# Operand scales from a ones matmul on TensorE in place of GpSimd's maximum over partitions

## The chip, the cores and the metric

The kernel runs on one core of a Trainium2 chip. The metric is the device time of one execution, in microseconds. Five engines work from instruction rows of their own: TensorE (PE, with its weight loads shown apart as PEld), VectorE (DVE), ScalarE (ACT), GpSimd (POOL) and SyncE (SP), which here issues most of the transfers.

## What is computed

One layer of a hybrid backbone over 2048 latent tokens of width 1024, with 256 context tokens, all float32:

```python
mod = silu(c) @ w_ada + b_ada                    # six shifts, scales and gates
h = rms_norm(x, norm1_g) * (1 + scale) + shift   # same for the context tokens
u, g, p, gt = split(h @ w_in)                    # LRU, GeLU gate, pool branch, branch gates
uc = depthwise_conv(u)
r, i = sigmoid(uc @ w_r + b_r), sigmoid(uc @ w_i + b_i)   # both directions, per head
out = scan(a(r), b(r, i, uc))                    # forward and backward, context state first
m = sigmoid(gt1) * ((out * gelu(g)) @ w_lru_out) + sigmoid(gt2) * (pool_mixer(p) @ w_pool_out)
x = x + gate * (m @ w_o)
h2 = rms_norm(x, norm2_g) * (1 + scale2) + shift2
x = x + gate2 * (square(relu(h2 @ w1)) @ w2)
y = rms_norm(x, final_g)
```

## The kernel before

Channels lie on the 128 partitions, tokens on the free dimension, in blocks of 512 tokens (b = 0 to 3). A float32 product is made of three float16 passes (`mm3`, L67 to L72, its matmuls are `mm` at L72): each operand is multiplied by a power of two, `s`, and split into a high and a low half (`split`, L93 to L95: the high half by ACT at L94, the low half by DVE at L95). The inverse scale goes into the evacuation.

The power of two comes from the operand's magnitude. DVE reduces each partition (`absmax`, L91, into `wm` for a weight chunk, `um` for an activation; two chunks that share a scale are joined into `wmj` at L114). `scale_of_` (L79 to L88) then makes one number of the 128: L81 is the maximum over partitions on POOL, into `sc_g`, L83 takes the exponent on DVE, L85 and L87 make the inverse `sc_inv` and the scale `sc_s`. There are 122 such calls: 69 for `wm`, 32 for `wmj`, 18 for `um` and 3 for `bd`, the bound of a modulated norm (`affine`, L340). The hidden activations of the MLP have a maximum over partitions of their own (`m1_split`, L837, `hm` at L841, 64 times), which the change leaves alone.

The other work of POOL is elementwise: the sums of squares of the first norms (L257), every second multiply of `modulate` (L237, tile `t` or `slot`), the products of input gates (L498), one step of the scans (L513), the sum of both directions (L535), and in the norms of the second half L217, L220 and L882.

The program runs in stages. The start (0 to 218 us) makes the adaLN vectors, the first norm and the first products. Eight LRU tiles of 128 channels follow (to about 916 us): the convolution (L471), `um` and its split, gate products, the scans (L521, L522), the GeLU gate, and between them, as `between`, the u products of the next tile, whose evacuation is L422, and part of the adaLN sums. Then come the pool branch (to 950), the branch products and the merge (to 1310; it reloads z and y from memory, into `B` and `yw`), the products with w_o and the second norm (`make_h2`, b = 3 last, at 1531 to 1602), and the MLP (16 groups of 256 hidden channels by 4 blocks, to the end), with the weights of the next group prepared meanwhile.

The order on SP is that of the code. On PE, DVE, ACT and POOL a scheduler sets it when the kernel is built, from its own time model; the blocks under `tc.high_priority` (`scale_of`, L76, among them) go first where they can. The order is fixed from then on, and each engine works its row in that order. TensorE's results of small sums, 512 columns at most, go to the PSUM pool `psm` (L60, tile `sm`), which has one buffer: the sum over partitions of squares by a ones matmul (`rstd`, L205), the adaLN sums (L401) and the last norm use it. `ones` (L133) is a 128x128 float32 tile of ones; L321 is a further ones matmul, of adaLN sums, into the pool of products.

Of the kernel before, what the change touches and what calls it, by code (L numbers as in the profile page):

```python
# [7 lines left out]
F32 = mybir.dt.float32  # L8
# [6 lines left out]
DRAM = bass.MemoryType.DRAM  # L15
ABSMAX = bass.bass_isa.ReduceOp.absmax

P = 128
# [3 lines left out]
BW = 512  # L22
# [19 lines left out]
def block_kernel(ctx: ExitStack, tc: tile.TileContext, a):  # L42
    """Activations keep channels on partitions and tokens on the free dimension.

    Matrix products run as three float16 passes (hi*hi + hi*lo + lo*hi) over operands that are
    scaled by powers of two taken from their measured magnitude and split into two halves.
    """
    nc = tc.nc
# [16 lines left out]

    # ---------------------------------------------------------------- helpers
    def mm3(ps, ws, xs):  # L67
# [11 lines left out]
    def scale_of_(m, k):  # L79
        g = sm.tile([P, k], F32, name=f"sc_g{k}")  # L80
        G.partition_all_reduce(g, m, P, ABSMAX)  # L81
        e = sm.tile([P, k], I32, name=f"sc_e{k}")
        V.tensor_scalar(e, g.bitcast(I32), 0x7F800000, None, op0=OP.bitwise_and)  # L83
        inv = sm.tile([P, k], F32, name=f"sc_inv{k}", bufs=8 if k == 1 else 4)
        V.tensor_scalar(inv.bitcast(I32), e, 14 << 23, 20 << 23, op0=OP.subtract, op1=OP.max)  # L85
        s = sm.tile([P, k], F32, name=f"sc_s{k}")
        V.tensor_scalar(s.bitcast(I32), inv.bitcast(I32), -1, 254 << 23, op0=OP.mult, op1=OP.add)  # L87
        return s, inv  # L88
# [13 lines left out]
    def prep(srcs, joint=False, w16=None):  # L102
        """Load chunks [128, n <= 1024]; each gets its own scale, or all of them one."""
        k = len(srcs)
        raws, m = [], sm.tile([P, k], F32, name=f"wm{k}")
        for i, src in enumerate(srcs):
            n = src.shape[-1]
            raw = ring.tile([P, 1024], F32, name="raw")
            nc.sync.dma_start(raw[:, :n], src)
            absmax(m[:, i:i + 1], raw[:, :n])  # L110
            raws.append(raw[:, :n])
        if joint:
            mj = sm.tile([P, 1], F32, name="wmj")
            V.tensor_reduce(mj, m, axis=AX.X, op=OP.max)  # L114
            m = mj
        s, inv = scale_of(m, 1 if joint else k)
        out = []
        for i, raw in enumerate(raws):
            n = raw.shape[-1]
            t = ring.tile([P, 2, 1024], F16, name="w16") if w16 is None else w16[i]  # L120
            split(t[:, 0, :n], t[:, 1, :n], raw, s[:, 0:1] if joint else s[:, i:i + 1])
            out.append(t)
        return out, inv
# [3 lines left out]

    # ---------------------------------------------------------------- constants and vectors
    vec = cp.tile([P, NV], F32, name="vec")
# [21 lines left out]

    # 8*softplus(-lam): max(-lam, 0) + log1p(exp(-|lam|)), log1p(e) = 2 atanh(e / (2 + e))
    nlam = cp.tile([P, 16], F32, name="nlam")
# [22 lines left out]

    # ---------------------------------------------------------------- scratch in DRAM
    z_d = [dram.tile([P, T], F32, name=f"z{j}") for j in range(KT)]
# [6 lines left out]

    # ================================================================ stages 0-3
    st = ExitStack()
# [14 lines left out]
    def rstd(total, w, rs):  # L202
        """1 / sqrt(mean + eps) on every partition of sums of squares [128, w] per partition."""
        ps = psm.tile([P, BW], F32, name="sm")
        TE.matmul(ps[:, :w], ones, total, start=True, stop=True)  # L205
        S.activation(rs, ps[:, :w], AF.Sqrt, bias=eps, scale=1.0 / D)
        V.reciprocal(rs, rs)
        return rs

    def rstd_of(x, w, t_tile):  # L210
        """The same of x [128, 8, w]."""
        acc = None
        for q in range(4):
            sq = ring.tile([P, 2, BW], F32, name="raw")[:, :, :w]
            S.activation(sq, x[:, 2 * q:2 * q + 2, :], AF.Square)
            if q:
                G.tensor_tensor(acc, acc, sq, op=OP.add)  # L217
            else:
                acc = sq
        G.tensor_tensor(acc[:, 0, :], acc[:, 0, :], acc[:, 1, :], op=OP.add)  # L220
        return rstd(acc[:, 0, :], w, t_tile()[:, :w])

    def pair(t, w=BW):
        """[128, k, w] float32 seen as [128, k, 2, w] float16: high and low halves in its place."""
        return t.bitcast(F16).rearrange("p k (h w) -> p k h w", h=2)

    def modulate(x, w, rs, gs, ss, dst, tmp):
        """x [128, 8, w] -> dst [128, 8, 2, w] (may be the same bytes)."""
        for k in range(KT):
            t = tmp()[:, :w]  # L230
            if k % 2 == 0:
                V.scalar_tensor_tensor(t, x[:, k, :], gs[:, k:k + 1], rs, op0=OP.mult, op1=OP.mult)
                S.activation(dst[:, k, 0, :], t, AF.Identity, bias=ss[:, k:k + 1])  # L233
                V.scalar_tensor_tensor(dst[:, k, 1, :], t, ss[:, k:k + 1], dst[:, k, 0, :],
                                       op0=OP.add, op1=OP.subtract)
            else:
                G.tensor_tensor(t, x[:, k, :], rs, op=OP.mult)  # L237
                S.activation(t, t, AF.Identity, bias=ss[:, k:k + 1], scale=gs[:, k:k + 1])
                S.activation(dst[:, k, 0, :], t, AF.Copy)
                V.tensor_tensor(dst[:, k, 1, :], t, dst[:, k, 0, :], op=OP.subtract)  # L240
# [8 lines left out]
    def norm_x(x, w, eng):  # L249
        """Its inverse root mean square and a supply of pieces, both in one slot."""  # L250
        t = slot([P, 4, BW])[:, :, :w]
# [24 lines left out]

    # shift1 and scale1 for the latent and the context stream
    w_ada = a["w_ada"].rearrange("(k p) n -> p k n", p=P)
# [16 lines left out]
    def ada1_pe(wt, cc):  # L295
        """As rows on two partitions, then turned into columns."""
        ps = ptile()
# [10 lines left out]
    def ada1_dve(wt, c):  # L308
        """Products summed over k on VectorE, then over partitions."""
        acc = slot([P, 512])  # L310
        for k in range(KT):
            if k == 0:
                V.tensor_scalar(acc, wt[k], sil[:, k, c:c + 1], None, op0=OP.mult)
            else:
                V.scalar_tensor_tensor(acc, wt[k], sil[:, k, c:c + 1], acc, op0=OP.mult, op1=OP.add)
        return acc
# [23 lines left out]
    def affine(scale, shift, g, m):  # L340
        """Scaled per-channel factor and term of a modulated norm, and the inverse scale."""
        gm = cp.tile([P, KT], F32, name=f"gm{m}")
# [41 lines left out]
    def ada_piece(q):  # L384
        """gate1, shift2, scale2, gate2 (q = 0..3) of the latent stream."""
        acc = slot([P, D])
# [20 lines left out]
    class Fill:  # L407
        """Sigmoid of one tile of branch-gate channels, kept in DRAM for the merge."""

# [23 lines left out]
    class Lru:  # L433
        """One tile of 128 recurrent channels: conv, gates, both scans, gelu gate."""

# [43 lines left out]
        def gates(self, between=()):  # L479
            """Recurrence and input gates; the products of other tiles go in between."""  # L480
            j, uc, u16, g16 = self.j, self.uc, self.u16, self.g16
# [57 lines left out]

    # first tiles, token block by token block as the normed input becomes ready  # L540
    def together(tiles, b):
# [77 lines left out]

    # ---------------------------------------------------------------- pool branch  # L620
    def rows(t, o=8, w=64):
# [73 lines left out]

    # ================================================================ branch outputs and merge
    st = ExitStack()
# [63 lines left out]

    # ================================================================ w_o, residual, second norm
    aff2 = affine(mod2[:, 2, :], mod2[:, 1, :], vc("g2"), 2)
# [47 lines left out]

    # ================================================================ squared-relu mlp
    st2.close()
# [73 lines left out]
    class FinishLast:  # L887
        """The same with the shortest way from the last product to the output."""

# [51 lines left out]

# [1 line left out]
def _tiles(w, cols):  # L943
    """[K, N] -> [128, K/128 * width] for a column range, k-tile major."""
    k, n = w.shape[0] // P, cols[1] - cols[0]
    return w[:, cols[0]:cols[1]].reshape(k, P, n).transpose(1, 0, 2).reshape(P, k * n)
# [54 lines left out]
```

## Time and profile before

| what | us |
|---|---|
| median of three runs | 2885.27 |
| lowest, highest | 2882.92, 2886.13 |
| the profiled execution: span | 2885.5 |
| TensorE busy in it | 2721.1 (94%) |
| DVE busy | 1904.9 (66%) |
| ACT busy | 812.7 (28%) |
| POOL busy | 459.1 (16%) |

The profile is of one execution, and its span lies within the runs. Busy time is summed over the whole span, though the stages differ: TensorE is full from the merge on, but for a few places, and has idle time ahead of it. A row of an instruction gives its start, its length and, in brackets, how long its engine idled before it and what ended that; "issue" is time in which the engine waited for nothing that the profile shows.

### The profile page before, as it was taken

How to read it: one execution, taken by the hardware profiler on the slowest of the kernel's cores; microseconds unless marked ns; L12 is line 12 of the kernel's file. 1: busy time of each engine (PE TensorE's matmuls, PEld its weight loads, DVE VectorE, ACT ScalarE, POOL GpSimd, SP SyncE). 2: the span in 40 equal slices, each digit the busy share in tenths (PEclk: the TensorE clock that was granted, in tenths of full speed). 3: DMA queues.
4: the chain of work that ended last, by engine and by line, in shares of the span. 5: the costliest groups of instructions: out<-in, count | busy, mean ns of one | idle time of the engine just before them, and what ended most of it. 6: DMA issues, size and time to landing. Idle time of an engine off the chain costs nothing.

```text
span 2885.5 us, 30620 instructions
## 1 busy us (share of the span) xinstructions
PE 2721.1 (94%) x12496; PEld 1241.8 (43%) x12496; DVE 1904.9 (66%) x2883; ACT 812.7 (28%) x917; POOL 459.1 (16%) x371
## 2 busy tenths in 40 slices
PE   5798988898889999999997999999999999999998
PEld 1344444444334444444443444444444444444444
DVE  4867778875576745676466666666666665656567
ACT  2655564446545232113231111011011110110112
POOL 2713332332322000000331000000000000000022
PEclk7899999999999999999999999999999999999999
DMA  7021123211111136433001000000000000000002
GB/s 304 9 77 59 70 99 113 88 51 55 55 41 40 55 121 222 154 105 132 30 18 56 30 30 29 16 30 25 20 30 30 30 16 29 30 22 23 0 30 88
DMA packets 49165, 177.60 MB, mean 62 GB/s; under 512 B 4736, under 2 KB 7040, under 8 KB 43520
## 3 DMA queue, kind: packets, MB, share of 16 engines
q1 hardware_dynamic: 44992, 146.29, 14.9%
q10 hardware_dynamic: 4032, 29.36, 2.5%
q8 instruction: 97, 1.59, 0.2%
q14 instruction: 44, 0.36, 0.0%
HBM read 137.88 MB, written 37.75 MB: 61 GB/s over the span
## 4 chain that ended last, share of the span: by engine, by line
PE 66%; DVE 13%; issue 7%; ACT 6%; POOL 5%; DMA 3%; SPq 0%; ACTq 0%; DVEq 0%; POOLq 0%
PE mm L72 65%; DVE slot L515 2%; POOL slot L513 2%; POOL sc_g L81 1%; DMA raw<-z 1%; DVE slot L518 1%; DVE slot L512 1%; DVE slot L395 1%; DVE wm L91 1%; POOL slot L535 1%; ACT slot L493 1%; DVE A L868 1%; DVE slot L471 1%; ACT slot L94 1%; POOL slot L257 1%
## 5 line engine op out<-in xcount | busy, mean ns | idle before, releaser
L72 PEld LDWEIGHTS <-w 128*128 128x128 f16 x10944 | 1078.1, 99 | 1387.2 <-issue 136.9
L72 PE MATMUL mm<-B,w 128*128 128x512 f16 x3840 | 845.6, 381 | 15.1 <-ACT B L233 5.3
L72 PE MATMUL mm<-A,w 128*128 128x512 f16 x3408 | 774.3, 388 | 72.2 <-ACT slot L422 56.8
L72 PE MATMUL mm<-h,w 128*128 128x512 f16 (+1 forms) x3120 | 676.4, 376 | 9.7 <-DVE h L858 9.5
L868 DVE SCALAR_TENSOR_TENSOR A<-mm,cs,A 128x512 f32<-128x512 f32 (+1 forms) x520 | 373.6, 738 | 44.2 <-PE mm L72 42.5
L833 DVE TENSOR_SCALAR_CACHE_REDUCE r<-mm 128x512 f32<-128x512 f32 x128 | 88.2, 689 | 309.8 <-PE mm L72 309.7
L855 ACT ACTIVATE h<-r 128x1024 f16<-128x1024 f32 x64 | 67.6, 1056 | 791.4 <-DVE ivs L850 766.0
L94 ACT ACTIVATE w<-raw,sc_s 128x1024 f16<-128x1024 f32 (+1 forms) x116 | 127.1, 1116 | 458.9 <-PE mm L72 260.2
L91 DVE TENSOR_REDUCE wm<-raw 128x1 f32<-128x1024 f32 (+1 forms) x124 | 146.2, 1181 | 123.9 <-DMA raw<-in_w_dram 78.5
L72 PE MATMUL mm<-B,yw 128*128 128x512 f16 x768 | 166.4, 379 | 0.0
L841 POOL PARTITION_ALL_REDUCE hm<-um x64 | 23.1, 361 | 865.9 <-DVE um L839 841.9
L95 DVE SCALAR_TENSOR_TENSOR w<-raw,sc_s,w 128x1024 f16<-128x1024 f32 (+1 forms) x116 | 143.1, 1253 | 26.7 <-ACT w L94 26.2
L72 PE MATMUL mm<-slot,g 128*128 128x512 f16 (+1 forms) x528 | 118.6, 373 | 4.9 <-ACT slot L493 4.9
L81 POOL PARTITION_ALL_REDUCE sc_g<-wm x69 | 65.6, 973 | 308.6 <-DVE wm L91 249.8
L72 PEld LDWEIGHTS <-yw 128*128 128x128 f16 x768 | 75.1, 98 | 91.6 <-issue 1.7
L493 ACT ACTIVATE slot<-mm,vec,ivg 128x512 f32<-128x512 f32 (+1 forms) x160 | 105.0, 743 | 10.9 <-PE mm L72 9.8
L498 POOL TENSOR_TENSOR slot<-slot 128x2312 f32<-128x2312 f32 x16 | 83.6, 5223 | 117.5 <-ACT slot L493 115.3
L94 ACT ACTIVATE slot<-slot,sc_s 128x2312 f16<-128x2312 f32 (+1 forms) x12 | 25.8, 2148 | 258.9 <-DVE sc_s L87 240.2
L512 DVE SCALAR_TENSOR_TENSOR slot<-slot 128x2312 f32<-128x2312 f32 x16 | 41.0, 2562 | 82.7 <-ACT slot L511 82.7
L72 PE MATMUL mm<-yw,w 128*128 128x512 f16 x384 | 83.4, 379 | 0.3 <-DVE w L95 0.2
L72 PEld LDWEIGHTS <-g 128*128 128x128 f16 x528 | 53.9, 102 | 65.5 <-issue 13.1
L858 DVE TENSOR_TENSOR h<-sq,h 128x1024 f16<-128x1024 f32 x64 | 77.9, 1217 | 0.0
(182 smaller groups left out, 2108.1 us busy)
## 6 DMA issues: line engine op xcount, KB each, us to landing
raw<-in_w_dram SPq DMA_DIRECT2D x64, 512.0 KB, 3.2
slot<-in_w_ada_dram SPq DMA_DIRECT2D x22, 1024.0 KB, 5.5
A<-in_xT_dram SPq DMA_DIRECT2D x8, 2048.0 KB, 8.7
t<-s SPq DMA_DIRECT2D x64, 256.0 KB, 3.5
s<-slot ACTq DMA_DIRECT2D x11, 1024.0 KB, 4.0
raw<-in_w_gt_dram SPq DMA_DIRECT2D x16, 512.0 KB, 7.2
z<-slot ACTq DMA_DIRECT2D x8, 1024.0 KB, 5.4
raw<-z SPq DMA_DIRECT2D x16, 512.0 KB, 5.8
```

The costliest lines, as they stand in the source:

```text
L72: TE.matmul(ps, l, r, start=(c == 0), stop=(c == n - 1))
L81: G.partition_all_reduce(g, m, P, ABSMAX)
L91: V.tensor_reduce(out, x, axis=AX.X, op=OP.max, apply_absolute_value=True)
L94: S.activation(hi, x, AF.Copy, scale=s)
L95: V.scalar_tensor_tensor(lo, x, s, hi, op0=OP.mult, op1=OP.subtract)
L493: S.activation(dst[:, o:o + w], ps[:, :w], AF.Sigmoid, bias=vcol("br" if i == 0 else "bi", 8 * d + j), scale=self.ivg)
L498: G.tensor_tensor(I, I, uc, op=OP.mult)
L512: V.scalar_tensor_tensor(Tt, A, 1.0, Tt, op0=OP.add, op1=OP.mult)
L833: V.tensor_scalar(r[:, i, :], ps, 0.0, None, op0=OP.max, op1=OP.max, accum_out=pm[:, i:i + 1])
L855: S.activation(h16[:, 0], r, AF.Square)
L858: V.tensor_tensor(h16[:, 1], sq, h16[:, 0], op=OP.subtract)
L868: V.scalar_tensor_tensor(x1[b][:, n, c], ps, cs[:, n:n + 1], x1[b][:, n, c], op0=OP.mult, op1=OP.add)
```

## The change

The maximum over partitions in `scale_of_` becomes a matmul of the 128x128 ones with the column of 128 partition maxima. TensorE adds up the maxima, and every partition of the PSUM tile holds the sum. So the scale comes from a sum of 128 magnitudes, which is at least their maximum and at most 128 times it; the rest of the scale's arithmetic is as before and reads PSUM. The tile comes from `psm`, whose one buffer it now shares with the norms' sums, the adaLN sums and the last norm. Comments are dropped elsewhere in the file; nothing else changes.

```diff
@@ scale_of_ (lines 79 to 88)
     def scale_of_(m, k):
-        g = sm.tile([P, k], F32, name=f"sc_g{k}")
-        G.partition_all_reduce(g, m, P, ABSMAX)
+        g = psm.tile([P, BW], F32, name="sm")[:, :k]
+        TE.matmul(g, ones, m, start=True, stop=True)
         e = sm.tile([P, k], I32, name=f"sc_e{k}")
         V.tensor_scalar(e, g.bitcast(I32), 0x7F800000, None, op0=OP.bitwise_and)
```

The change leaves SP's order alone. POOL's row goes from 365 entries to 164 and TensorE's from 24614 to 24736. Three places show the order.

POOL at the second norm of the last block, `make_h2(3)`, before. An ISA row with `sc_g` or `hm` is a maximum over partitions; one that names no tile stands wherever POOL goes over from elementwise work to maxima or back:

```order
L237 ISA
L237 TENSOR_TENSOR t_10237<-A_9481,t_10227 128x512
L81 ISA
L81 ISA sc_g_10948<-wmj 128x1
L237 ISA
L237 TENSOR_TENSOR t_10246<-A_9481,t_10227 128x512
L81 ISA
L81 ISA sc_g_10975<-wmj 128x1
L237 ISA
L237 TENSOR_TENSOR t_10255<-A_9481,t_10227 128x512
L841 ISA
L841 ISA hm<-um 128x1
```

The same place after:

```order
L841 ISA
L841 ISA hm<-um 128x1 x2
L237 ISA
L237 TENSOR_TENSOR t_10237<-A_9481,t_10227 128x512
L237 TENSOR_TENSOR t_10246<-A_9481,t_10227 128x512
L237 TENSOR_TENSOR t_10255<-A_9481,t_10227 128x512
L237 TENSOR_TENSOR t_10264<-A_9481,t_10227 128x512
L841 ISA
L841 ISA hm<-um 128x1 x57
```

The four multiplies of L237 stand together now, and the maxima of weights between them are gone.

TensorE at the first LRU tile, before: `w_1088` is the weight of fill products, `g_1108` that of the first gate products, which need the split of `um`'s operand:

```order
L72 MATMUL mm<-A_358,w_1088 128x512
L72 LDWEIGHTS g_1108
L72 MATMUL mm<-slot,g_1108 128x512
L72 LDWEIGHTS g_1108
L72 MATMUL mm<-slot,g_1108 128x512
L72 LDWEIGHTS g_1108
L72 MATMUL mm<-slot,g_1108 128x512
```

The same place after, where `um` and four `wm` are columns of partition maxima:

```order
L72 LDWEIGHTS w_1088
L72 MATMUL mm<-A_358,w_1088 128x512
L81 MATMUL sm<-um,ones 128x1
L81 MATMUL sm<-wm_1249,ones 128x1
L81 MATMUL sm<-wm_1529,ones 128x1
L81 MATMUL sm<-wm_1544,ones 128x1
L81 MATMUL sm<-wm_1562,ones 128x1
L72 LDWEIGHTS g_1108
L72 MATMUL mm<-slot,g_1108 128x512
L72 LDWEIGHTS g_1108
```

Five ones matmuls, `um` and four of weights, now stand in one row between the fill products and the first gate product.

TensorE late in the merge, as a difference, with `yw` the pool branch's output and `w_7501` a weight chunk; `wm_7578` belongs to the chunk of the next products, those of z:

```order
 L72 LDWEIGHTS w_7501
 L72 MATMUL mm<-yw,w_7501 128x512
+L81 MATMUL sm<-wm_7578,ones 128x1
 L72 LDWEIGHTS w_7501
 L72 MATMUL mm<-yw,w_7501 128x512
```

The ones matmul is put between two products of the chunk before, which stood one behind the other.

## Rows read from the trace of the kernel before

**Rows 1.** The page: busy tenths of TensorE and GpSimd in 40 slices of 72 us

```profile
PE   5798988898889999999997999999999999999998
...
POOL 2713332332322000000331000000000000000022
```

**Rows 2.** The page: the chain that ended last, its shares of the span by engine

```profile
PE 66%; DVE 13%; issue 7%; ACT 6%; POOL 5%; DMA 3%; SPq 0%; ACTq 0%; DVEq 0%; POOLq 0%
```

**Rows 3.** Stretches: length, busy time of each engine, granted clock, DMA share, GB/s

```profile
72.00:144.00 72.00, 57.54 (x229) 24.09 (x228) 64.31 (x51) 45.03 (x73) 54.07 (x37) 0.90 0.03 10
648.00:720.00 72.00, 62.74 (x292) 29.15 (x292) 41.83 (x42) 48.49 (x50) 19.07 (x11) 0.93 0.15 55
1152.00:1224.00 72.00, 68.31 (x303) 29.68 (x301) 50.74 (x88) 15.32 (x14) 4.43 (x8) 0.95 0.49 160
1512.00:1584.00 72.00, 55.94 (x250) 24.72 (x248) 45.95 (x89) 14.81 (x18) 11.27 (x12) 0.94 0.18 59
```

**Rows 4.** The chain in order of time, 0 to 216 us: start, us, what

```profile
162.60 0.79 PE mm L321 x8
```

**Rows 5.** Instructions of POOL, 1540 to 1605 us: start, us, instruction, idle before

```profile
1545.22 1.59 POOL L237 TENSOR_TENSOR t<-A,t 128x512 f32<-128x512 f32 x1 [7.17 <-DVE wm L91]
...
1552.54 0.96 POOL L81 PARTITION_ALL_REDUCE sc_g<-wmj  x1 [5.73 <-DVE wm L91]
...
1560.89 1.25 POOL L237 TENSOR_TENSOR t<-A,t 128x512 f32<-128x512 f32 x1 [7.39 <-issue]
...
1590.09 1.25 POOL L237 TENSOR_TENSOR t<-A,t 128x512 f32<-128x512 f32 x1 [7.03 <-DVE A L868]
```

**Rows 6.** TensorE by group, 1531 to 1602 us: busy, mean ns, idle before

```profile
L72 PE MATMUL mm<-h,w 128*128 128x512 f16 x106 | 25.1, 394 | 9.7 <-DVE h L858 9.5 <-DVE A L868 0.2
L72 PE MATMUL mm<-B,w 128*128 128x512 f16 x98 | 24.9, 415 | 11.7 <-ACT B L233 5.3 <-DVE B L234 4.9 <-DVE A L868 1.5
L205 PE MATMUL sm<-raw,ones 128*128 128x512 f32 x2 | 1.0, 592 | 0.0
```

**Rows 7.** Instructions of DVE and POOL around the first norm's bound

```profile
56.76 0.16 DVE L347 SCALAR_TENSOR_TENSOR bd<-bd 128x1 f32<-128x1 f32 x1
...
65.20 0.41 POOL L81 PARTITION_ALL_REDUCE sc_g<-bd  x1 [5.81 <-issue]
```

**Rows 8.** Instructions of DVE and TensorE around the first tile's um

```profile
192.69 2.56 DVE L91 TENSOR_REDUCE um<-slot 128x1 f32<-128x2312 f32 x1
...
202.12 1.03 PE L72 MATMUL mm<-slot,g 128*128 128x512 f16 x4
```

**Rows 9.** Instructions of DVE and POOL in the second LRU tile

```profile
361.81 2.55 DVE L91 TENSOR_REDUCE um<-slot 128x1 f32<-128x2312 f32 x1
...
364.50 0.67 POOL L81 PARTITION_ALL_REDUCE sc_g<-um  x1 [10.22 <-DVE um L91]
...
380.19 5.21 POOL L535 TENSOR_TENSOR slot<-slot 128x2048 f32<-128x2048 f32 x1 [10.56 <-DVE slot L395]
```

**Rows 10.** Waits of TensorE, whole span: us in total, times, longest

```profile
PE mm L72 <- ACT slot L422: 56.8, 7, 9.5
...
PE mm L72 <- ACT w L94: 6.6, 2, 3.5
```

**Rows 11.** Instructions of POOL and DVE in the sixth LRU tile

```profile
667.44 0.41 POOL L81 PARTITION_ALL_REDUCE sc_g<-wm  x1 [6.24 <-issue]
...
667.88 0.15 DVE L83 TENSOR_SCALAR sc_e<-sc_g 128x1 int32<-128x1 int32 x1 [12.36 <-POOL sc_g L81]
```

**Rows 12.** Instructions of DVE and TensorE late in the merge

```profile
1159.81 10.10 PE L72 MATMUL mm<-yw,w 128*128 128x512 f16 x46 [0.18 <-DVE w L95]
...
1168.80 1.21 DVE L91 TENSOR_REDUCE wm<-raw 128x1 f32<-128x1024 f32 x1
...
1173.03 1.03 PE L72 MATMUL mm<-B,w 128*128 128x512 f16 x2 [3.12 <-ACT w L94]
```

**Rows 13.** One joint maximum on DVE in the MLP

```profile
2634.41 0.15 DVE L114 TENSOR_REDUCE wmj<-wm 128x1 f32<-128x2 f32 x1
```

## The prediction

> **What bounds the kernel now.** I read the page's busy slices first [rows 1]: TensorE is full in all but the first twenty or so of forty slices, and there GpSimd (POOL) has the digits that TensorE lacks. The chain of work that ended last says the same in shares: TensorE 66%, but 7% "issue" and 5% POOL [rows 2]. So a microsecond is only won where TensorE idles, and TensorE time that is added where it is full is paid one for one. The table of stretches sorts the places: 62.74 of 72 us are busy in an LRU tile, 68.31 in the merge, 55.94 in the second norm, and 72.00 in the MLP [rows 3].
>
> The partition maximum is itself cheap: 0.41 us for one column at 65.20 [rows 7]. What costs is POOL's change of work around it. In the second norm L237 and L81 alternate, and each begins 5.73 to 7.39 us after the one before has ended, called "issue" or put down to something long done [rows 5]. In the order of instructions an ISA row without a tile stands at each such change, so I read the gaps as the price of a change. [...]
>
> **The change part by part.** 122 reductions leave POOL, and with them most of its changes of work; 122 ones-matmuls enter TensorE's row, in planned places; scalar work on DVE stays, and SP's order doesn't move. I walk the program by stages, gains positive.
>
> *Added TensorE time.* One ones-matmul is two passes of a float32 matmul. The nearest row is L321, the same ones and one moving column: eight passes, four matmuls, held the chain for 0.79 us [rows 4], so 0.20 us each; a handover from and to float16 weights may add a little, and a float32 pass of 512 columns on the same weights, 592 ns [rows 6], bounds a pair from above at 1.2. I take 0.23 us, near the one-column row, and as the upper end 0.5, since one column streams where that row has 512. By the new order 70 of the 122 stand where TensorE is full (the merge and all behind it): 70 x 0.23 = **-16 us** (-14 to -35). The other 52 lie where TensorE idles anyway.
>
> *Second norm, make_h2(3), 1531 to 1602 us.* Here MLP products wait for h2 and for the hidden scales. [...] POOL goes through seven such changes between 1538 and 1601; the group shows four [rows 5]. The new order has two: into L237, four norm multiplies in a row, and back. The multiplies then end near 1552, not at 1591.34 [rows 5]. What is late next is the one change that is left, 7.2 us, of which I let 4 reach TensorE. 25 - 4 = **+21 us** (15 to 26).
>
> *Start, 0 to 218 us.* POOL's changes lie on the chain there. The bound for the first norm's factors, bd, is reduced by 56.9 and its maximum starts at 65.20, behind 5.81 us of "issue" [rows 7]; two changes before it delay POOL's part of the norm as well. Without them I put the factors 13 us earlier, the 8 us between those rows and 5 for one change ahead of them. Most of it is lost again. DVE is busy 64.31 of the 72 us from 72 to 144 [rows 3], so the shift ends in its queue. And the first tile's um ends at 195.25 [rows 8], but its ones-matmul stands behind all fill products, at the place that TensorE reaches at 202.12 [rows 8], and four more stand directly behind it; they share one PSUM buffer, so each waits until DVE has read the one before. With the split behind it (2.2 us on ACT, 2.63 on DVE) some 6 us of the gates' start is lost, and 4 more at the context product, whose ones-matmul stands behind other work as well. 13 - 10 = **+3 us** (0 to +10).
>
> *LRU tiles 1 to 4.* Each has a POOL gap before um's maximum (10.22 us idle, put down to um) and one before L535 (10.56) [rows 9]. The first is hidden: um ends at 364.36, the maximum starts at 364.50 [rows 9]. The second only holds the sum of the two scans, whose users come later. Now TensorE stands at um's ones-matmul 5 to 8 us before um is there, but it idles up to 9.5 us right behind it anyway (56.8 us at seven places [rows 10]), so that is neutral. +1 each = **+4 us** (-8 to +20, the upper end if half of L535's wait comes back).
>
> *LRU tiles 5 to 7.* There a second change sits on the path: the maximum of the next weights runs at 667.44 after 6.24 us of "issue", and DVE has been idle 12.36 us for it [rows 11]. Without POOL's changes that wait goes; next late are the weight transfers and the scan's activations, so I keep 3.5 of the 12.36: 3 x 3.5 = **+10 us** (0 to 37, all of it).
>
> *Pool branch and merge.* ACT's weight split held TensorE twice before, 6.6 us in all [rows 10]. Now the ones-matmul stands earlier in TensorE's row than the split's user. In the pool branch the um matmul stands behind 288 products, and I give that **-2.5 us** (-6 to 0, the longest of the two stalls again and a little). In the merge one reduction ends at 1170.01 [rows 12], while its matmul's place, 13 products after 1159.81, is reached near 1162.6 [rows 12]: TensorE stops 7.4 us. Before, it did the 33 products behind that place (7.1 us) and then idled 3.12 [rows 12]. Now those 33 run after the stop, beside the 3 us of scale and split: 7.4 - 3.1 = **-4 us** (-7 to 0).
>
> *MLP.* The joint maximum stands on DVE 3 us before TensorE comes to its matmul (2634.41 [rows 13] against 2637.7 by count of products, and 2.4 to 3.4 for the others), and the scale is used much later. No stall, so nothing beyond the 0.23.
>
> Sum: -16 + 21 + 3 + 4 + 10 - 2.5 - 4 = +15.5 us. The profiled execution's span is 2885.5 us, the median of the runs 2885.27, so both can be set equal: 2885.5 - 15.5 = **2870 us**.
>
> **The rivals.** *TensorE's strict row* (slower). An ones-matmul that waits holds every product behind it, and there is one buffer. I counted the stalls of 5 to 8 us in the seven LRU tiles as covered by idle time behind them [rows 10]. If half of that cover is gone because the tile is DVE's and ACT's chain and um itself comes no earlier, 7 x 3.3 = 23 us are lost and the +14 of the tiles goes with it: 2870 + 37 = 2907, and about 2895 if a third is lost and half of the gain stays. It decides the sign once the LRU tiles together lose more than about 7 us. For it: um, not POOL, ends last at 364.36; against it: 9 us idle per 72 in those tiles [rows 3]. [...]
>
> *The tiles give the whole wait back* (faster). If transfers and DVE follow, tiles 5 to 7 gain 25 us more than I took, less some that ACT holds, and L535 a few in the others: 2870 - 30 = 2840. For it: 12.36 us of DVE idle time behind one instruction. Against it: ACT's own work of a tile, and the scans, don't shrink.
>
> [...]
>
> **How the numbers follow.** Forecast 0.43 (2858 to 2879), the strict row 0.22, whole wait back 0.16, no change 0.19. No measurement of this kernel tells less than 0.2%, about 5.8 us, from nothing: the borders are 2879.5 and 2891. Faster 0.43 + 0.16 + 0.01 of the rest = 0.60, same 0.20, slower 0.20. The range leaves out the upper half of the strict row and the lower half of the full gain: 2842 to 2900.
>
> **What would show it.** Right: no POOL gap over 5 us between 1555 and 1595 and TensorE busy over 66 in 1512 to 1584; DVE's 12.36 us at L83 gone in tiles 5 to 7; the stretches of the MLP longer by 0.23 us for each ones-matmul; a stop of some 7 us at L81 near the end of the merge. [...]

## The result, and the profile after

The changed kernel takes 2838.76 us, the median of four runs (2836.59 to 2840.46), against 2885.7 for the kernel before: ratio 0.9839, 95% interval 0.9825 to 0.9853. That is 46.9 us or 1.6% less, three times the 15.5 that were forecast, and 3 us below the range. The profiled execution of after was its fastest, with a span of 2834.4 us, so differences that are read from the two traces add up to 51.1 us.

The page of after, the same parts as [rows 1] and [rows 2] (busy tenths of TensorE and GpSimd, the chain's shares):

```profile
PE   6898898888989999999999999999999999999998
...
POOL 5512222222221000000231000000000000000032
...
PE 75%; DVE 13%; ACT 5%; issue 2%; POOL 2%; DMA 2%; SPq 0%; DVEq 0%; ACTq 0%; POOLq 0%
```

In the first half four of TensorE's slices are a digit higher and two a digit lower, and the 22nd, with the second norm in it, goes from 7 to 9. The chain's "issue" is 2% where it was 7%, POOL 2% where it was 5%. The stretches that answer to three of [rows 3], moved to where the same work now stands (us, busy time of each engine, granted clock, DMA share, GB/s):

```profile
600.00:672.00 72.00, 63.23 (x307) 30.35 (x306) 51.03 (x46) 43.32 (x47) 17.86 (x8) 0.93 0.16 60
...
1118.00:1190.00 72.00, 70.51 (x337) 32.89 (x336) 50.66 (x88) 13.67 (x13) 0.00 (x0) 1.00 0.46 146
...
1480.00:1552.00 72.00, 69.79 (x326) 32.06 (x325) 61.63 (x115) 21.21 (x25) 11.81 (x10) 1.00 0.19 61
```

In the stretch from the LRU tiles TensorE is hardly fuller, 63.23 against 62.74 us, but a tile has become shorter: from the reduction of `um` in tile 5 to that in tile 6 it takes 85.1 us (614.53 to 699.61), before 91.9 (641.05 to 732.98). In the merge TensorE is busy for 70.51 us against 68.31, and POOL has no work in this stretch. At the second norm it is 69.79 against 55.94 at a granted clock of 1.00. TensorE's longest waits before ones matmuls, with the one of [rows 10] that is left (us in total, times, longest):

```profile
PE sm L81 <- DVE um L91: 56.5, 7, 9.1
...
PE sm L81 <- DVE wm L91: 9.8, 3, 7.2
...
PE mm L72 <- ACT w L94: 4.8, 1, 4.8
...
PE sm L81 <- DVE sc_e L83: 3.5, 9, 0.9
```

The 7.2 us in the second row are the first weights, 7 us into the program. The 56.8 us at seven places that TensorE waited for L422's evacuation are now 56.5 us at the seven ones matmuls of um. The products behind such a ones matmul waited with it, up to 9.1 us. But the idle time only changed its place.

Where the gain lies can be read from the start of the n-th float16 product in both traces, since both run the same 12288 of them; where the order differs a little, from the same instruction. LRU tiles are numbered from 0 here, as in the prediction; the tile of [rows 9], called the second there, is tile 2. The lead of after changes like this:

| step | forecast, us | in the traces, us |
|---|---|---|
| start, up to the second tile's um | +3 | +16.9 |
| LRU tiles 1 to 4 | +4 | +9.6 |
| LRU tiles 5 to 7 | +10 | +16.3 |
| pool branch | -2.5 | -3.3 |
| merge and products with w_o, without the ones matmuls' own time | -4 | -2.8 |
| added TensorE time, 70 ones matmuls | -16 | -9.6 |
| second norm, make_h2(3), likewise | +21 | +23.9 |
| sum | +15.5 | +51.0 |

A row is good to some 3 us: from the end of the LRU tiles to the second norm, traces of the experiments below that have all their maxima there on POOL, as before, still move by -0.6 to +4.3 us against the trace of before.

### The profile page after: what moved, and what is told of

Same layout as the page of the kernel before. It is cut to its first block, busy times and chain, and to the rows that moved or that the text cites. A ratio compares the mean times of both kernels' runs of the same rounds, so it can differ in the third digit from the quotient of the medians.

```text
span 2834.4 us, 30824 instructions
## 1 busy us (share of the span) xinstructions
PE 2717.8 (96%) x12740; PEld 1263.2 (45%) x12740; DVE 1915.9 (68%) x2883; ACT 814.2 (29%) x917; POOL 367.9 (13%) x249
## 4 chain that ended last, share of the span: by engine, by line
PE 75%; DVE 13%; ACT 5%; issue 2%; POOL 2%; DMA 2%; SPq 0%; DVEq 0%; ACTq 0%; POOLq 0%
PE mm L72 73%; DVE slot L515 2%; DVE slot L471 1%; POOL slot L513 1%; DVE slot L514 1%; DVE slot L518 1%; DVE slot L512 1%; ACT slot L493 1%; DMA raw<-z 1%; DVE wm L91 1%; ACT slot L510 1%; ACT slot L509 1%; DVE um L91 1%; DVE w L95 1%; ACT slot L511 1%
## 5 line engine op out<-in xcount | busy, mean ns | idle before, releaser
L94 ACT ACTIVATE w<-raw,sc_s 128x1024 f16<-128x1024 f32 (+1 forms) x116 | 127.2, 1116 | 400.4 <-PE mm L72 268.7
L95 DVE SCALAR_TENSOR_TENSOR w<-raw,sc_s,w 128x1024 f16<-128x1024 f32 (+1 forms) x116 | 151.8, 1323 | 48.2 <-ACT w L94 47.5
L217 POOL TENSOR_TENSOR raw<-raw 128x1024 f32<-128x1024 f32 x21 | 51.0, 2429 | 457.9 <-ACT raw L215 442.4
L94 ACT ACTIVATE slot<-slot,sc_s 128x2312 f16<-128x2312 f32 (+1 forms) x12 | 25.8, 2149 | 242.7 <-DVE sc_s L87 242.7
L857 DVE TENSOR_TENSOR sq<-r 128x1024 f32<-128x1024 f32 x64 | 77.8, 1215 | 0.0
```

What stands on the lines that cost most here:

```text
L94: S.activation(hi, x, AF.Copy, scale=s)
L95: V.scalar_tensor_tensor(lo, x, s, hi, op0=OP.mult, op1=OP.subtract)
L857: V.tensor_tensor(sq, r, r, op=OP.mult)
```

## Experiments

Each experiment is compared with the kernel before on the same chip; the times before were 2884.5 to 2885.5 us in all of them. The order on the engines is planned anew for each, so places can move beyond the edit. Most choose by the number of the scale call in the code, counted from 1, whether the column goes to TensorE or to POOL:

```diff
-        g = psm.tile([P, BW], F32, name="sm")[:, :k]
-        TE.matmul(g, ones, m, start=True, stop=True)
+        calls[0] += 1
+        if calls[0] <= 11:
+            g = psm.tile([P, BW], F32, name="sm")[:, :k]
+            TE.matmul(g, ones, m, start=True, stop=True)
+        else:
+            g = sm.tile([P, k], F32, name=f"sc_g{k}")
+            G.partition_all_reduce(g, m, P, ABSMAX)
```

The lines are set against the changed kernel; one more, `calls = [0]`, stands ahead of them. The line numbers of these kernels are six higher behind it (L87 is the maximum, L541 the sum of the scans, L243 the multiplies of L237); the ones matmul is L84.

### Four parts alone

Start (`calls[0] <= 11`):

> The ones matmul in the first eleven scale calls alone (the start, and the first LRU tile's own), GpSimd's maximum everywhere else. Theory A, GpSimd's changes of work delay elementwise work that is on the path, stage by stage, and the stages add up: the two traces stand 16.9 us apart when the second tile's um is reduced, so this gives about -17 us against the kernel before (2869). Theory B, the tiles behind have a chain of their own and swallow what the start gives, so that the gain shows only together with theirs: less than 8 us.

LRU tiles (`11 < calls[0] <= 48`):

> The ones matmul in the LRU tiles alone (calls 12 to 48). Theory A: the traces move apart by another 25.9 us between the second tile's um and the pool branch, so -26 us (2860). Theory B, part of that came from transfers that an earlier start had put ahead: less than 15 us.

Pool branch, merge and splits for w_o (`48 < calls[0] <= 90`):

> The ones matmul in the pool branch, the merge and the splits for w_o alone (calls 49 to 90). Theory A, TensorE stops at ones matmuls whose column is late and pays 0.137 us for each of the others: the traces come together by 11.1 us here, so +11 us (2897). Theory B, the merge is bound by its transfers, and what it lost is part of the lead that it came with: then it loses under 4 us when it starts no earlier.

MLP weights (`calls[0] > 90`):

> The ones matmul for the joint scales of the MLP weights alone (calls 91 to 122). Theory A: 23.3 us won at make_h2(3), where GpSimd no longer goes back and forth, less 28 ones matmuls of 0.137: -19 us (2866). Theory B, the norm was late because of what came before it: under 8 us.

Measured: 2878.6 (ratio 0.9977, interval 0.9966 to 0.9988), 2861.0 (0.9913, 0.9896 to 0.993), 2905.35 (1.007, 1.0053 to 1.0086) and 2864.3 us (0.9926, 0.9908 to 0.9944). So -6.4, -24.0, +20.3 and -20.7 us. The tiles and the MLP gave what the traces had shown. The start gave little more than a third, the merge lost nearly twice as much, and their sum is -30.8, not -46.9. Both misses have a place in their traces. POOL's instructions in the start kernel (start, us, instruction, idle before):

```profile
167.06 0.41 POOL L87 PARTITION_ALL_REDUCE sc_g<-wm  x1 [6.53 <-DVE sc_s L93]
...
174.73 0.71 POOL L243 TENSOR_TENSOR slot<-hc,slot 128x256 f32<-128x256 f32 x1 [7.26 <-issue]
...
181.16 0.88 POOL L87 PARTITION_ALL_REDUCE sc_g<-wm  x2 [5.71 <-issue]
```

The first product was 14.5 us earlier, but the maxima for the weights of the next tile, whose calls were left on POOL, stand in between the context stream's multiplies, and POOL changes its work three times here, 6.53, 7.26 and 5.71 us. The lead, 17.6 us at the context product, is 1.8 when the gates run. In the merge kernel one ones matmul of a later stage was planned into an LRU tile ahead of its data:

```profile
764.88 0.56 PE L84 MATMUL sm<-wm,ones 128*128 128x1 f32 x2 [11.81 <-DVE wm L97]
```

TensorE waits 11.81 us for it, the strict row of the rivals as it was described, only in a kernel that was not forecast; by the end of the tiles 6 of them are lost for good. Its pool branch and merge lose 12 us, as theory A had it, so the merge isn't simply held by its transfers. Another 6.3 us go at about 1455 us, ahead of the norms: a maximum of `wmj`, still POOL's, stands between the norm's sums of squares, TensorE comes to wait 3.3 us for POOL's L226 (L220 before), and behind the wait products ran at a granted clock of 0.52 over 6 us (1458 to 1464).

To settle the start, the limit was moved behind the weights of the next tile (`calls[0] <= 14`):

> The ones matmul in the first 14 scale calls, three more than in the first experiment: the weights of the next tile, which GpSimd worked on in between the context stream's multiplies there. GpSimd then has no change of work up to the second tile. Theory A, a stage gives its gain only if no change of work is left in it: -16.9 us (2868), all of it kept behind. Theory B, the tiles swallow what the start gives: under 8 us, as with 11 calls.

2867.49 us, ratio 0.9946 (0.9926 to 0.9965): -17.6 us, and the lead in the trace is 17 us at the gates and 24 at the end. Theory B falls. The start gives its gain when the changes between the multiplies are gone, not call by call.

### The change of work without the wait

The changed kernel, with POOL's maxima back beside the matmuls, their results unread:

```diff
         TE.matmul(g, ones, m, start=True, stop=True)
+        G.partition_all_reduce(sm.tile([P, k], F32, name=f"sc_g{k}"), m, P, ABSMAX)
```

> The changed kernel, with GpSimd's maximum over partitions put back beside every ones matmul; nothing reads what it gives, so GpSimd changes its work as often as before, but no scale waits for it. Theory A, the delay of the elementwise work behind such a change was what cost time: most of the gain goes, at make_h2(3) all of it, and the time is 2870 to 2890. Theory C, the wait of the scale for the maximum was what cost time: the gain stays, 2835 to 2845.

2886.38 us, ratio 1.0005 (0.9993 to 1.0017): in sum the whole gain is gone, though no scale waits for POOL. By stages it isn't the kernel before again. In its trace, 3.3 us behind before's, and with the ones matmuls' own time, the start is 7.2 us behind (the changed kernel is 16.9 ahead), the tiles win 5.6 (25.9), the stretch from the pool branch to the products with w_o loses 16.1 (11.5), the second norm wins 17.9 (23.4), and the MLP loses 3.6 (3.6). So all of the gain in the start and most of it in the tiles went when the maxima came back, unread. In the start TensorE waits for sums of squares, the longest two times for such that stand behind a change on POOL (L258 is L257 before; us in total, times, longest):

```profile
PE sm L206 <- POOL slot L258: 20.7, 3, 11.6
```

In seven tiles POOL changes its work ahead of the sum of the scans again, as before. At the second norm theory A's "all of it" missed. POOL there (L238 are the multiplies, L237 before):

```profile
1558.19 1.26 POOL L238 TENSOR_TENSOR t<-A,t 128x512 f32<-128x512 f32 x1 [7.92 <-DVE sc_e L84]
...
1565.29 0.41 POOL L82 PARTITION_ALL_REDUCE sc_g<-wmj  x1 [5.84 <-DVE t L233]
...
1572.70 1.26 POOL L238 TENSOR_TENSOR t<-A,t 128x512 f32<-128x512 f32 x1 [7.00 <-issue]
1576.27 1.71 POOL L238 TENSOR_TENSOR t<-A,t 128x512 f32<-128x512 f32 x1 [2.31 <-DVE B L241]
...
1582.41 1.71 POOL L238 TENSOR_TENSOR t<-A,t 128x512 f32<-128x512 f32 x1 [4.43 <-DVE B L241]
...
1590.01 0.97 POOL L842 PARTITION_ALL_REDUCE hm<-um  x1 [5.89 <-DVE wm L92]
```

The order of this kernel has three of the four multiplies in a row, so two changes into them and not four as before [rows 5], and TensorE idles 6.1 us there, not the 21.4 of before (9.7 and 11.7 [rows 6]). So at the second norm this run doesn't separate the delay of the multiplies from the wait of a scale; that the maxima of `wmj` between them were the cause is shown by the kernel with the MLP weights alone.

### What holds an LRU tile

The ones matmul for um alone in seven tiles, and for the weights alone:

```diff
+        if calls[0] in (15, 20, 25, 30, 35, 40, 45):                                # um
+        if 11 < calls[0] <= 48 and calls[0] not in (15, 20, 25, 30, 35, 40, 45):    # weights
```

> In LRU tiles 1 to 7 the ones matmul for um alone (7 calls), GpSimd's maximum for the weights. Theory A: the weights' maxima still make GpSimd change its work in each tile, so little of the 24 us of the tiles comes: 0 to 8 us. Theory D, each call that leaves GpSimd saves its own wait, and um's is the longest: 12 us or more.

> The counterpart: in LRU tiles 1 to 7 the ones matmul for the weights (30 calls), GpSimd's maximum for um. Theory A: um's maximum stands ahead of L535 in each tile and keeps one change, but the second change, ahead of the weights in tiles 5 to 7, is gone: 5 to 15 us. Theory D: 24 us less what um alone gave.

um alone: 2861.41 us, ratio 0.9921 (0.9905 to 0.9936), -23.7 us, all that the tiles give. The weights alone, 30 of the 37 calls: 2881.55, ratio 0.9989 (0.9979 to 0.9998), -3.5 us. Theory A in the form that I gave it, any change left spoils the tile, is wrong: both traces have 48 changes on POOL where before has 62, and one has all of the gain, the other next to none. What counts is what stands behind a change. In the trace with um on TensorE the weights' maxima still change POOL's work, but behind L541, not ahead of it:

```profile
639.00 4.52 POOL L541 TENSOR_TENSOR slot<-slot 128x2048 f32<-128x2048 f32 x1 [15.29 <-DVE sc_e L89]
...
649.42 0.41 POOL L87 PARTITION_ALL_REDUCE sc_g<-wm  x1 [5.90 <-issue]
```

In the kernel before, the change stood between um's maximum and L535, and the chain through a tile runs over it (start, us, what):

```profile
364.50 5.14 POOL sc_g L81 x2
...
380.19 5.21 POOL slot L535
...
385.84 6.82 DMA raw<-in_w_gl_dram
...
392.68 1.22 DVE wm L91
...
406.22 2.21 ACT slot L509
```

L535 starts 15.7 us behind the start of um's maximum, 10.56 of them idle. The row of [rows 9] puts this down to DVE's L395; but in the kernel with unread maxima, where that step ended 2.7 to 3.1 us before the sum of the scans, the idle time in tiles 1 to 4 is 9.6 to 10.4 us as well, called "issue". Why it is some 3 us longer there than the 7.1 to 7.3 of tiles 5 to 7 stays open. SP's next transfers wait in front of POOL's small memsets, which stand behind L535 in POOL's row (SP's waits, 380 to 390 us):

```profile
SPq L389 <- POOL slot L445: 15.1, 1, 15.1
```

The transfer of the next weights follows at 385.84, the reduction of the weights at 392.68, and the scan's activations at 406.22. That leaves two readings: um's scale, or L535. The kernel before with L535 on DVE tells them apart:

```diff
-            G.tensor_tensor(z[:, 0:T], self.h[0][:, 0:T], z[:, 0:T], op=OP.add)
+            V.tensor_tensor(z[:, 0:T], self.h[0][:, 0:T], z[:, 0:T], op=OP.add)
```

> The kernel before, all maxima on GpSimd, with the sum of the two scans (L535) moved from GpSimd to DVE, so that GpSimd has no change of work between um's maximum and the next tile's. Theory F, L535 behind GpSimd's change is what held the tile, since the transfers of the next weights wait for the buffers behind it: most of the tiles' 24 us comes without any ones matmul, less 2.3 us of DVE in each of seven tiles as far as DVE is on the path, -10 to -24 us. Theory D, um's scale waiting for its maximum held the tile: no gain, 0 to +16 us.

2861.81 us, ratio 0.9914 (0.9894 to 0.9933): -22.7 us with every maximum on POOL. Theory F holds. Tile 2 of this kernel (DVE's row of L535, then POOL's):

```profile
365.84 2.28 DVE L535 TENSOR_TENSOR slot<-slot 128x2048 f32<-128x2048 f32 x1
...
361.20 4.54 POOL L81 PARTITION_ALL_REDUCE sc_g<-wm  x1
...
378.13 0.10 POOL L443 MEMSET slot<- 128x2 f32 x1 [12.39 <-DVE slot L395]
```

L535 follows the scan at 365.84 and ends at 368.12, 7.5 us behind the start of um's maximum (360.61), before 20.9 (385.40). POOL's memsets still wait, now for a DVE step of the adaLN sums, but start 17.5 us behind um's maximum and not 20.9: 3.3 us in a tile, 23 in seven. This kernel takes L535's own 5.2 us off POOL together with the change; the one with um alone on TensorE takes away the change only, and wins the same.

### The price of one, and a better mixture

Each ones matmul twice, into the same buffer:

> The changed kernel, every ones matmul issued twice into the same buffer. By the traces one costs TensorE 0.137 us where it is full, so the 70 there give +9.6 us over the changed kernel (2848), and nothing or little in the stages before; by the 0.23 us of the prediction +16 (2855).

2862.87 us, ratio 0.9923 (0.9908 to 0.9938): 24.1 us above the changed kernel, more than either figure. In the MLP of the changed kernel (TensorE's rows):

```profile
2304.09 2.75 PE L72 MATMUL mm<-B,w 128*128 128x512 f16 x12
...
2306.68 0.28 PE L81 MATMUL sm<-wmj,ones 128*128 128x1 f32 x2
...
2306.82 7.93 PE L72 MATMUL mm<-B,w 128*128 128x512 f16 x36
```

and of this one (its L82 is the second matmul):

```profile
2329.45 0.28 PE L81 MATMUL sm<-wmj,ones 128*128 128x1 f32 x2
...
2329.59 0.36 PE L82 MATMUL sm<-wmj,ones 128*128 128x1 f32 x2
...
2329.81 7.93 PE L72 MATMUL mm<-B,w 128*128 128x512 f16 x36
```

One ones matmul moves the next product by 0.14 us, two by 0.36. A second one right behind costs 0.22, about the size of the L321 row from which I took my price. By the lead in the traces, 5.8 us more are lost behind the second norm (some 25 calls of 0.22), 12.6 from the pool branch to the products with w_o, where longer stops join, and 6.3 up to the end of the LRU tiles. The expectation of little there was wrong.

The ones matmul where it wins, and POOL's maximum where POOL has little else to do (`calls[0] <= 49 or 90 < calls[0] <= 96`):

> The ones matmul up to the end of the LRU tiles (49 calls) and around make_h2(3) (calls 91 to 96), GpSimd's maximum in the pool branch, the merge, the splits for w_o and the rest of the MLP. Theory A, the stages add up: the changed kernel without the 11 us that it loses in the merge and 26 x 0.137 = 3.6 in the MLP, 2824. Theory B, the merge is bound by its transfers and takes back what it is ahead: 2835 to 2840.

2822.71 us, ratio 0.9785 (0.977 to 0.9799), 16 us better than the changed kernel and 62.8 better than before, with 15 changes of work left on POOL. The lead stays at 40.6 us from the pool branch to the end of the merge, so theory B falls here too. The same with the first tile's um on POOL (`and calls[0] != 10`):

> The mixed kernel (2822.7), with GpSimd's maximum for the um of the first LRU tile alone. There TensorE has many products ahead of the ones matmul's place, so that um's scale waits for the place and not for um; GpSimd's changes before and after it fall into idle time. As the prediction had it, the gates then start 5 to 6 us earlier: 2817. Theory E, the gates' start is set by something else (the split, the weights of the gates): no change.

2821.21 us, ratio 0.978 (0.9765 to 0.9796). Not to be told from the mixture, so theory E. TensorE there (first row: with the maximum on POOL; the others: the mixture):

```profile
185.98 1.86 PE L73 MATMUL mm<-slot,g 128*128 128x512 f16 x4 [0.87 <-ACT slot L100]
...
182.95 0.28 PE L84 MATMUL sm<-um,ones 128*128 128x1 f32 x2
...
186.27 1.87 PE L73 MATMUL mm<-slot,g 128*128 128x512 f16 x4
```

The gate products start at 185.98 and 186.27; with the maximum on POOL it is ACT's split (L100, L94 before) that they wait for last. And the hidden scales on TensorE as well:

```diff
-        gm = sm.tile([P, 1], F32, name="hm")
-        G.partition_all_reduce(gm, mx, P, ABSMAX)
+        gm = psm.tile([P, BW], F32, name="sm")[:, :1]
+        TE.matmul(gm, ones, mx, start=True, stop=True)
```

> The changed kernel, with the ones matmul also for the scale of the hidden activations, 64 times in the MLP, so that GpSimd has no maximum over partitions left. Theory A: the one change that is left at make_h2(3) goes (3 to 4 us back), and 64 x 0.137 = 8.8 us of TensorE come on top, +5 us (2844). The strict row: each of the 64 stands behind products that end only just before its column is there, and TensorE stops 0.5 to 1.5 us at each, +35 to +95 us.

2848.15 us, ratio 0.9874 (0.9857 to 0.9891): 9.4 us above the changed kernel, about 64 x 0.14, and no stops. Nothing came back at the second norm, where TensorE now waits for ACT:

```profile
PE mm L72 <- ACT h L855: 2.7, 1, 2.7
```

## Why the prediction was wrong

The sign, the mechanism at the second norm and the two losses were right; the size was a third of the gain. The time lay nearest to the second rival, the tiles that give the whole wait back (2840), but that is luck: that rival has all of 30 us more from the tiles, and they gave 11.9 more than forecast, the start 13.9.

**Second norm: right in the row and the size.** +23.9 against +21. Four multiplies in a row, one change into them and one back (POOL in after):

```profile
1509.08 1.26 POOL L237 TENSOR_TENSOR t<-A,t 128x512 f32<-128x512 f32 x1 [7.71 <-DVE sc_e L83]
...
1514.77 1.27 POOL L237 TENSOR_TENSOR t<-A,t 128x512 f32<-128x512 f32 x1 [4.43 <-DVE B L234]
...
1521.91 1.71 POOL L237 TENSOR_TENSOR t<-A,t 128x512 f32<-128x512 f32 x1 [5.87 <-DVE B L240]
...
1528.05 1.72 POOL L237 TENSOR_TENSOR t<-A,t 128x512 f32<-128x512 f32 x1 [4.43 <-DVE B L240]
...
1535.81 0.81 POOL L841 PARTITION_ALL_REDUCE hm<-um  x1 [6.05 <-DVE A L868]
```

They end at 1529.77, with 4.43 to 5.87 us between them that DVE sets: with the 31.2 us added by which the stage starts earlier that is 1561, not the 1552 of the prediction. TensorE's groups there, to be read against [rows 6]:

```profile
L72 PE MATMUL mm<-B,w 128*128 128x512 f16 x172 | 38.0, 379 | 0.6 <-DVE A L868 0.6
...
L72 PE MATMUL mm<-h,w 128*128 128x512 f16 x144 | 32.0, 379 | 1.6 <-ACT h L855 1.4 <-DVE h L858 0.2
...
L81 PE MATMUL sm<-wmj,ones 128*128 128x1 f32 x8 | 1.1, 208 | 0.0
```

The 21.4 us of idle time are 2.2, and a product takes 379 ns on average, not 394 or 415. No run shows by itself the other 4 us of the forecast's 25, for slower products. What the traces show in their place: before, the granted clock was 0.86 over the stage (1531 to 1602) and 0.50 from 1583 to 1595, after, it was 1.00 from 1488 to 1560; from the means, 106 x 15 ns and 98 x 36 ns, I estimate some 5 us. That the 4 us I let remain were due to the last change was not so: without it, in the kernel with hidden scales on TensorE, 2.7 us of waiting for ACT remain.

**The start: the step that failed most,** +16.9 against +3. The factors were indeed earlier. POOL and TensorE before (a POOL row, and the first float16 product):

```profile
20.04 9.30 POOL L257 TENSOR_TENSOR slot<-slot 128x512 f32<-128x512 f32 x7 [11.26 <-issue]
...
69.16 1.01 PE L548 MATMUL mm<-A,w 128*128 128x512 f16 x2 [14.04 <-ACT A L233]
```

and after:

```profile
12.70 9.32 POOL L257 TENSOR_TENSOR slot<-slot 128x512 f32<-128x512 f32 x7 [12.27 <-ACT slot L255]
...
50.33 0.59 PE L81 MATMUL sm<-bd,ones 128*128 128x1 f32 x2 [4.70 <-DVE bd L347]
...
54.06 1.01 PE L548 MATMUL mm<-A,w 128*128 128x512 f16 x2 [1.48 <-ACT A L233]
```

bd's scale comes 14.9 us earlier (50.33 against [rows 7]), the first product 15.1 us. By 140 us on the clock of before the lead is 22; a later change of POOL on the way there, ahead of the sums at 72.99 us with 6.70 us idle, is gone too. I had 13, and then took 10 off for DVE's queue, the place of the first um's matmul and the context product. Of these 10, some 5 showed: 2 at the context product, and 3.3 where the five ones matmuls stand in a row between fill and gate products (181.80 to 185.10). DVE's queue was no wall: busy 64 of 72 us [rows 3], the stretch moved forward as a whole, and the first um's reduction starts 14.7 us earlier (177.96). The um's matmul waited 1.3 us for its place (um ready at 180.52, matmul at 181.80), not 7, since TensorE's fill products had moved forward as well, and the experiment with that um on POOL gained nothing that can be measured. So the term should have been some 22 - 5, not 13 - 10. I had read places from the new order and times from the old trace, and shifted one of the two.

**LRU tiles 1 to 4:** +9.6 against +4. The failing sentence is that L535 "only holds the sum of the two scans, whose users come later". SP's transfers wait behind it, and the chain of before runs over it. In the changed kernel L535 of tile 2 starts 4.5 us behind the end of um's reduction (351.29 against 346.81), before 15.8. **Tiles 5 to 7:** +16.3 against +10. There I saw a wait on the path and put it down to the second change, ahead of the weights [rows 11]; the runs show that the first, ahead of L535, was the one: weights alone on TensorE gave 3.5 us for all seven tiles, um alone 23.7, and L535 on DVE, with every maximum on POOL, 22.7. I did not ask who is queued on other engines behind a late elementwise instruction.

**The strict row,** a rival with 0.22: the stops came, 56.5 us of them, and cost nothing, since they took the place of others of the same length [rows 10]. That part of the prediction was right. Where a matmul was planned ahead of its data in the kernel with the merge alone, 6 of the 11.8 us were lost.

**Pool branch and merge: right in size** as far as the traces tell, -3.3 and -2.8. But the stop of 7.4 us at `wm_7578` didn't come: the reduction ended 38.3 us earlier, at 1131.68, and the matmul's place came only 30 us earlier, at 1132.60, so that it found the column ready. What was lost is shorter stops and the clock after one: at 1108 us a stop of about 2 us is followed by products at twice the pitch, 0.43 us and not 0.22:

```profile
1108.00:1113.00 5.00, 4.91 (x16) 2.04 (x17) 4.45 (x10) 0.72 (x1) 0.00 (x0) 0.66 0.32 77
```

The granted clock was 0.66 over these 5 us, and 0.50 from 1109 to 1112.

**Added TensorE time: the term was mis-sized,** 0.14 us for each in place of 0.23, 6.4 us over 70. That TensorE is full in the MLP, which the prediction reads from a stretch that [rows 3] doesn't show, is so in this one of before:

```profile
2376.00:2448.00 72.00, 72.00 (x336) 32.61 (x334) 44.52 (x88) 7.66 (x7) 1.78 (x5) 1.00 0.09 30
```

The L321 row has four matmuls behind one another, and the kernel has single ones between float16 products.

That POOL's change of work takes time was read from ISA rows and gaps. The trace had instructions of it by name on the sequencer of POOL (the count, durations in ns, first and last start in us, of L535 in the kernel before):

```profile
L535 POOLq MODIFY_POOL_CONFIG  x14: 83/83/83, 276.1 to 833.6; - x14
```

Each change has two such rows; there are 124 of them in the trace before, for 62 changes, and 26 in the trace after. In the trace before, from the first of the two to the next instruction it took 5.5 us or more into a maximum and 6.7 or more into elementwise work. The fastest kernels here leave this maximum to POOL only where POOL has little else to do: with the maximum on POOL in the merge and the ones matmul up to the end of the tiles and around the second norm 2822.7 us, against 2885 with the maximum everywhere.

## What to carry to other kernels

Where an engine takes time to change its work, as POOL did here (5.5 us or more into a maximum), look before pricing an operation at what stands behind it in that engine's row and who waits for that, also the queue that issues transfers; one reduction in a tile can cost as much as all of them (um alone gave 23.7 us, all calls of the tiles 24.0). Move the uses away that put a change ahead of such work (in the tiles 7 calls of 37 gave the whole gain, in the start three calls left behind took more than half of it), and leave them where the engine has little other work. When an order after a change is read against a trace before it, let both sides move: a stage that starts earlier brings its waiters along.

## What the runs showed that was not expected

A float32 ones matmul with one moving column costs 0.14 us alone between float16 products and 0.22 more when another stands right behind it. Maxima over partitions whose results nobody reads made the changed kernel 47.6 us slower (2886.4 against 2838.8 us). A change of work on POOL took at least 5.5 us into a maximum and 6.7 into elementwise work, and some 10 us ahead of L535 in four tiles. And a stop of some 2 us in the merge was followed by products at a granted clock of 0.66 over 5 us.
